# The triangular inverses' substitution on GpSimd instead of VectorE, in an encoder trunk with three mixers

## The chip, the cores and the metric

One core of one Trainium2 chip runs the whole kernel. The metric is the device time of one execution in microseconds, as the median of several runs. The engines are TensorE (PE, with its weight loads PEld), VectorE (DVE), ScalarE (ACT), GpSimd (POOL) and the DMA queues (SP issues them).

## The reference

One layer of a trunk on 1024 tokens of width 1024. A normalised and modulated input is projected by one wide matrix (82 tiles of 128 columns). Three branches read the projection: an mLSTM matrix memory, a Hyena long convolution, and RWKV-7 time mixing. Each has a gate; the three are projected, merged and projected again. What matters here is the third:

```
def step(state, inp):                       # per head, 64 x 64 state, 16 heads, both directions
    r_t, w_t, k_t, v_t, kk_t, a_t = inp
    sa = einsum('bhij,bhj->bhi', state, -kk_t)
    state = (state * w_t[:, :, None, :] + sa[..., None] * (kk_t * a_t)[:, :, None, :]
             + v_t[..., None] * k_t[:, :, None, :])
    return state, einsum('bhij,bhj->bhi', state, r_t)
```

Each token's update reads the state that the one before it left. All is float32.

## The kernel before

The kernel runs in stages: the modulated input is made, then the mLSTM branch, the Hyena branch, the RWKV branch, and the merge with the output projection. The projection is cut into jobs, one for each 128 columns. A job loads its weight tile in four parts (`load_w`): a DMA into `wraw`, a cast to the high half `wh` on ScalarE, and the difference `wl`, the low half, on GpSimd (L334). Its matmuls (`gemm`, L351 to L353) write `pg`, three for each of 8 row blocks and each half of the tokens. There are three `wraw` buffers and four each of `wh` and `wl`, which is one tile's weights. The jobs are handed out piece by piece among the other stages' work.

RWKV does not go token by token. It takes two heads at a time (8 pairs of heads), and of a pair 16 chunks of 64 tokens, forward and backward at once. Within a chunk the dependence of the tokens on each other is a triangular system of 64 by 64. Its inverse is made ahead by `tphase`, for 8 chunks of both directions together (a half, `g`), so there are two calls for each pair and 16 in all. A call works as follows:

- TensorE forms the triangular products `pq`; ScalarE copies the 32 by 32 blocks of the diagonal to `quad` and the block under it to `q21`.
- VectorE transposes `quad` to `Ab` (L1625), so that each of 128 partitions holds one 32 by 32 triangle. A DMA fills `Tb` with identities (L1628).
- The substitution, 31 steps (L1630 to L1636): step `l` makes the outer product `tm` of column `l` of `Ab` with row `l` of `Tb`, and adds it to the rows of `Tb` below. A step has 31 - l rows and l // 2 + 1 columns; the 31 products have 16 to 136 elements each in a partition, 2856 in all. Each product reads what the sum before it wrote, and each sum reads its product.
- VectorE transposes `Tb` back into `t1` and `t2` (L1641, L1644). TensorE then makes the block under the diagonal by two rounds of small products into `pwx`, with a copy `W` between, and ScalarE copies the parts into `tt`.

`scan` (L1740) then goes through the chunks. A step multiplies by the inverse and carries the state on: a group of products into `pch`, a copy `us` on VectorE (L1769), products with `tt`, copies into `SV` on VectorE and ScalarE, products with `B`, two sums `sn` on VectorE, and again copies into `SV`. One `us` thus stands for one step. Half of the chunks' `tt` is used by 8 steps.

Beside the scan, `weave` places the preparation of the next pair (`prep`, which makes `ar` and `bk` from `tmp`, `s`, `a`), the next half's `tphase`, the end of the pair before (`post`) and the projection jobs. Within a `tphase` there is a `yield` after every fifth step of the substitution, and the generators run under a raised priority (`ahead`, 400 places). A scheduler then orders each engine's queue from the dependences, the priorities and its own costs; each queue is worked off strictly in that order.

Of the kernel before, what the change touches and what calls it, by code (L numbers as in the profile page):

```python
# [28 lines left out]
MUL, ADD, SUB, MAX, MIN = ALU.mult, ALU.add, ALU.subtract, ALU.max, ALU.min  # L29
# [256 lines left out]
class Trunk:  # L286
# [1310 lines left out]
    def tphase(self, cx, g):  # L1597

        nc, rp = self.nc, self.rp
        x2 = lambda n: self.ep.tile([128, 16, 32], F32, name=n, tag="x2", bufs=3)
        q, q21 = x2("quad"), self.ep.tile([128, 16, 32], F32, name="q21", tag="q21", bufs=1)
        pq = [x.rearrange("p (c t) -> p c t", t=CL) for x in self.banks("pq")]

        def blocks():

            for d in range(2):
                for c in range(8):
                    bt, al = cx["bk"][g, d, c], cx["ar"][g, d, c]  # L1610
                    for h in range(2):
                        hs = slice(64 * h, 64 * h + 64)
                        yield partial(nc.tensor.matmul, pq[d][64 * h:64 * h + 32, c, :], bt[hs, 0, 0:32], al[hs, 0, :],
                                      start=True, stop=True)
                        yield partial(nc.tensor.matmul, pq[d][64 * h + 32:64 * h + 64, c, 0:32], bt[hs, 0, 32:64],
                                      al[hs, 0, 32:64], start=True, stop=True)
        self.in_turn(blocks())
        for d, ps in enumerate(pq):
            u = slice(d * 8, d * 8 + 8)
            nc.scalar.copy(q[:, u, :], ps[:, :, 0:32])  # L1620
            for h in range(2):
                nc.scalar.copy(q21[64 * h:64 * h + 32, u, :], ps[64 * h:64 * h + 32, :, 32:64])
        yield
        Ab = self.ep.tile([128, 32, 32], F32, name="Ab", tag="Ab", bufs=1)
        nc.vector.transpose(Ab.rearrange("p t (g u) -> p t g u", g=2),  # L1625
                            q.rearrange("p u t -> p t u").unsqueeze(2).broadcast_to([128, 32, 2, 16]))
        Tb = x2("Tb").rearrange("p a b -> p (a b)").rearrange("p (t s) -> p t s", s=16)
        nc.sync.dma_start(Tb, self.A["tinit"])  # L1628
        tm = rp.tile([128, 136], F32, name="tm", tag="tm", bufs=1)
        for l in range(31):  # L1630
            n, m = 31 - l, l // 2 + 1
            x = tm[:, 0:n * m].rearrange("p (a b) -> p a b", b=m)
            self.tt(x, Ab[:, l + 1:32, l].unsqueeze(2).broadcast_to([128, n, m]),
                    Tb[:, l, 0:m].unsqueeze(1).broadcast_to([128, n, m]))
            o = Tb[:, l + 1:32, 0:m]
            self.tt(o, o, x, ADD)  # L1636
            if l % 5 == 4:
                yield
        tt = self.tt_t[g]
        t1 = x2("t1").rearrange("p a b -> p (a b)").rearrange("p (v s) -> p v s", s=16)  # L1640
        nc.vector.transpose(t1.rearrange("p v s -> p s v"), Tb.rearrange("p t s -> p s t"))  # L1641
        t1 = t1.rearrange("p (g u) s -> p u s g", g=2)
        t2 = x2("t2")
        nc.vector.transpose(t2.rearrange("p u (s g) -> p u s g", g=2), t1)  # L1644
        yield

        W = x2("W")
        pw, px = (x.rearrange("p (u t) -> p u t", t=32) for x in self.banks("pwx"))
        r = [slice(64 * h, 64 * h + 32) for h in range(2)]
        self.in_turn(partial(nc.tensor.matmul, pw[64 * h + 32:64 * h + 64, u, :], q21[r[h], u, :], t1[r[h], u, :],  # L1650
                             start=True, stop=True) for u in range(16) for h in range(2))
        for h in range(2):
            r1, r2 = slice(64 * h, 64 * h + 32), slice(64 * h + 32, 64 * h + 64)
            nc.scalar.copy(W[r2], pw[r2])
            nc.scalar.copy(tt[r1, :, 0:32], t2[r1])
            nc.scalar.copy(tt[r2, :, 32:64], t2[r2])
        yield
        r = [slice(64 * h + 32, 64 * h + 64) for h in range(2)]
        self.in_turn(partial(nc.tensor.matmul, px[64 * h:64 * h + 32, u, :], W[r[h], u, :], t2[r[h], u, :],
                             start=True, stop=True) for u in range(16) for h in (1, 0))  # L1660
        for h in range(2):
            r1 = slice(64 * h, 64 * h + 32)
            nc.scalar.copy(tt[r1, :, 32:64], px[r1])
        yield
# [251 lines left out]
```

## Time and profile before

| | |
|---|---|
| median of 3 runs | 2187.35 us (2179.21 to 2191.44) |
| the profiled execution | 2200.05 us; its span 2198.3 us |
| mean granted clock of TensorE | 0.956 |
| busy: PE, DVE, ACT, POOL | 1994.0, 1634.6, 1103.2, 424.3 us |
| products tm, 496 on VectorE | 145.4 us, mean 293 ns |
| sums Tb, 496 on VectorE | 144.2 us, mean 291 ns |
| splits wl, 408 on GpSimd | 371.5 us, mean 915 ns |

The span is from the first to the last instruction of one execution. A group's line gives the source line, the engine, the operation, the tiles written and read, the shape and count; then the busy time and the mean of one, and the idle time of the engine just before its instructions with what ended it. L476 and L473 are helpers for VectorE, so the tiles' names tell what is meant. A row of the timeline starts with the start and the duration in microseconds.

### The profile page before, as it was taken

The numbers are of one execution on the slowest core, as the hardware profiler recorded it, in microseconds if no ns is written. First come the engines' busy times: TensorE is split into PE (matmuls) and PEld (weight loads), VectorE is DVE, ScalarE is ACT, GpSimd is POOL, SyncE is SP. The second block draws the span as 40 slices with busy tenths as digits, with TensorE's granted clock in tenths as the row PEclk, the third lists the DMA queues.
The fourth block names the chain that finished last, engine by engine and source line by source line (L and its number), as shares of the span: only waits on it lengthen the run. The fifth ranks groups of instructions, "written<-read, shape, count | busy, mean of one in ns | idle before, by whom it ended". The sixth has DMA issues, their size and how long they took to land. (4 is left out here: it accounts for less than half of the span.)

```text
span 2198.3 us, 45984 instructions
## 1 busy us (share of the span) xinstructions
PE 1994.0 (91%) x17098; PEld 1509.2 (69%) x17098; DVE 1634.6 (74%) x4754; ACT 1103.2 (50%) x2558; POOL 424.3 (19%) x485
## 2 busy tenths in 40 slices
PE   6999899999989899899989999999898887897998
PEld 4666777787868677666766676666666665675786
DVE  4854999988447947788787888868887888764536
ACT  5557356454242115664665756667466564532221
POOL 2211311122222432311101111111114411010200
PEclk9999999999999999999998999999899998897999
DMA  8211222334465345321322333224143542445623
GB/s 255 70 67 59 78 77 90 112 101 127 143 200 172 119 138 163 124 68 61 130 79 93 117 106 102 92 81 136 52 155 118 187 144 63 159 143 175 196 89 129
DMA packets 169384, 262.19 MB, mean 119 GB/s; under 512 B 17863, under 2 KB 87335, under 8 KB 169160
## 3 DMA queue, kind: packets, MB, share of 16 engines
q1 hardware_dynamic: 169160, 259.25, 36.3%
q8 instruction: 135, 2.21, 0.4%
q14 instruction: 89, 0.73, 0.1%
HBM read 181.06 MB, written 78.12 MB: 118 GB/s over the span
## 5 line engine op out<-in xcount | busy, mean ns | idle before, releaser
L334 POOL TENSOR_TENSOR wl<-wraw,wh 128x256 fp32r<-128x256 f32 x408 | 371.5, 915 | 1488.6 <-ACT wh L333 1464.8
L351 PE MATMUL pg<-hh,wh 128*128 128x512 f32 x1440 | 601.5, 418 | 20.9 <-ACT wh L333 11.8
L352 PE MATMUL pg<-hh,wl 128*128 128x512 f32 x1440 | 594.3, 413 | 16.4 <-POOL wl L334 16.3
L353 PE MATMUL pg<-hl,wh 128*128 128x512 f32 x1440 | 592.4, 412 | 1.9 <-DVE hl L565 1.8
L351 PEld LDWEIGHTS pg<-hh,wh 128*128 128x128 f32 x1440 | 278.7, 194 | 88.9 <-ACT wh L333 15.1
L352 PEld LDWEIGHTS pg<-hh,wl 128*128 128x128 f32 x1440 | 279.3, 194 | 78.0 <-POOL wl L334 22.2
L353 PEld LDWEIGHTS pg<-hl,wh 128*128 128x128 f32 x1440 | 278.1, 193 | 62.0 <-DVE hl L565 2.8
L333 ACT CAST wh<-wraw 128x256 fp32r<-128x256 f32 x408 | 162.7, 404 | 220.6 <-PE pg L353 122.1
L476 DVE TENSOR_TENSOR tm<-Ab,Tb 128x126 f32<-128x126 f32 (+22 forms) x496 | 145.4, 293 | 4.4 <-DMA Tb<-in_tinit 2.7
L476 DVE TENSOR_TENSOR Tb<-Tb,tm 128x126 f32<-128x126 f32 (+22 forms) x496 | 144.2, 291 | 1.9
L473 DVE SCALAR_TENSOR_TENSOR st<-pg,hmu,st 128x511 f32<-128x511 f32 (+1 forms) x130 | 80.9, 636 | 27.9 <-ACT e L424 17.6
L476 DVE TENSOR_TENSOR G<-pgr,gmask 128x512 f32<-128x512 f32 x128 | 85.4, 679 | 17.0 <-PE pgr L398 17.0
L457 ACT ACTIVATE st<-pg 128x512 f32<-128x512 f32 x74 | 44.2, 597 | 99.9 <-PE pg L353 95.0
L1684 ACT COPY G<-ar 64x128 f32<-64x128 f32 x256 | 64.3, 295 | 48.4 <-DVE G L476 46.6
L473 DVE SCALAR_TENSOR_TENSOR st<-st,pg 128x512 f32<-128x512 f32 x80 | 54.3, 679 | 35.7 <-PE pg L353 12.7
L398 PE MATMUL pgr<-ar,bk 64*128 64x128 f32 x896 | 76.9, 287 | 0.0
L141 DVE SCALAR_TENSOR_TENSOR row<-row 64x1 f32<-64x1 f32 x393 | 72.7, 208 | 2.1
L1769 DVE COPY us<-pch 128x128 f32<-128x128 f32 x128 | 36.3, 283 | 45.8 <-PE pch L398 45.5
L395 PEld LDWEIGHTS pch<-SV,G 128*64 128x64 f32 x256 | 25.3, 139 | 65.5 <-ACT SV L1801 52.3
L395 PE MATMUL pch<-SV,G 128*64 128x64 f32 x256 | 43.2, 252 | 27.7 <-ACT SV L1801 26.2
L476 DVE TENSOR_TENSOR dw<-dw,dw 128x512 f32<-128x512 f32 x92 | 67.1, 760 | 0.9
L395 PEld LDWEIGHTS pch<-SV,B 128*64 128x64 f32 x256 | 25.3, 139 | 60.1 <-ACT SV L1776 50.1
(677 smaller groups left out, 4228.4 us busy)
## 6 DMA issues: line engine op xcount, KB each, us to landing
wraw<-in_w_in SPq DMA_DIRECT2D x340, 128.0 KB, 2.3
low<-lora SPq DMA_DIRECT2D x32, 512.0 KB, 4.1
sig<-st SPq DMA_DIRECT2D x48, 256.0 KB, 2.6
st<-sig SPq DMA_DIRECT2D x48, 256.0 KB, 3.5
wraw<-in_w_br SPq DMA_DIRECT2D x68, 128.0 KB, 2.8
adw<-in_ada_w SPq DMA_DIRECT2D x16, 512.0 KB, 7.1
x<-in_x SPq DMA_DIRECT2D x8, 512.0 KB, 6.1
hx<-st SPq DMA_DIRECT2D x16, 256.0 KB, 2.0
```

The source lines that it names most:

```text
L141: self.ops.append(lambda: self.nc.vector.scalar_tensor_tensor(o, a, s, b, op0=op0, op1=op1))
L333: self.nc.scalar.copy(hi, raw)
L334: self.nc.gpsimd.tensor_tensor(lo, raw, hi.bitcast(F32), op=SUB)
L351: nc.tensor.matmul(p, wh, hh, start=(k == 0), stop=False)
L352: nc.tensor.matmul(p, wl, hh, start=False, stop=False)
L353: nc.tensor.matmul(p, wh, hl, start=False, stop=(k == n - 1))
L395: ins = f()
L398: ins = f()
L457: self.nc.scalar.activation(o, p, AF.Tanh, scale=0.5)
L473: return self.nc.vector.scalar_tensor_tensor(out, in0, s, in1, op0=op0, op1=op1)
L476: return self.nc.vector.tensor_tensor(out, a, b, op=op)
L1684: nc.scalar.copy(G[0:64, :, d, h, 0:64], cx["al"][g, d, b % 4][hsl[h]])
```

## The change

The product and the sum of each step are issued on GpSimd and not on VectorE. Nothing else of the source is changed.

```
         for l in range(31):
             n, m = 31 - l, l // 2 + 1
             x = tm[:, 0:n * m].rearrange("p (a b) -> p a b", b=m)
-            self.tt(x, Ab[:, l + 1:32, l].unsqueeze(2).broadcast_to([128, n, m]),
-                    Tb[:, l, 0:m].unsqueeze(1).broadcast_to([128, n, m]))
+            nc.gpsimd.tensor_tensor(x, Ab[:, l + 1:32, l].unsqueeze(2).broadcast_to([128, n, m]),
+                                    Tb[:, l, 0:m].unsqueeze(1).broadcast_to([128, n, m]), op=MUL)
             o = Tb[:, l + 1:32, 0:m]
-            self.tt(o, o, x, ADD)
+            nc.gpsimd.tensor_tensor(o, o, x, op=ADD)
             if l % 5 == 4:
                 yield
```

The scheduler's order of all engines moves with it. On VectorE, the end of the third substitution and the transposes that follow it stood thus before:

```order
L476 TENSOR_TENSOR Tb_10427<-Tb_10427,tm_10429 128x3x15
L476 TENSOR_TENSOR sn_10858<-pch_10774,sn_10722 128x128
L476 TENSOR_TENSOR tm_10429<-Ab_10425,Tb_10427 128x30
L476 TENSOR_TENSOR bk_11068<-a_10997,s_10995 128x4x64
L476 TENSOR_TENSOR Tb_10427<-Tb_10427,tm_10429 128x2x15
L476 TENSOR_TENSOR sn_10858<-sn_10858,pc_9071 128x128
L476 TENSOR_TENSOR tm_10429<-Ab_10425,Tb_10427 128x16
L476 TENSOR_TENSOR hsp_11133<-mm_9628,hsp_11133 128x512
L476 TENSOR_TENSOR Tb_10427<-Tb_10427,tm_10429 128x16
L1800 COPY SV_9264<-sn_10858 64x2x64
L1641 STREAM_TRANSPOSE t1_10702<-Tb_10427 128x16x32
L1769 COPY us_10891<-pch_10882 128x128
```

Here one instruction of other work stood between a product and its sum. The same transpose, with what stands before and behind it in VectorE's queue, now:

```order
L1800 COPY SV_9620<-sn_10444 64x2x64
L476 TENSOR_TENSOR bk_10634<-tmp_10389,s_10386 128x4x64
L476 TENSOR_TENSOR bk_10634<-a_10388,s_10386 128x4x64
L1769 COPY us_10490<-pch_10481 128x128
L476 TENSOR_TENSOR bk_10990<-tmp_10389,s_10386 128x4x64
L476 TENSOR_TENSOR bk_10990<-a_10388,s_10386 128x4x64
L1775 COPY SV_9620<-pch_10481 64x2x64
L1641 STREAM_TRANSPOSE t1_10702<-Tb_10427 128x16x32
L476 TENSOR_TENSOR y_9270<-y_9270,pch_10363 128x64
L1644 STREAM_TRANSPOSE t2_10704<-t1_10702 128x512
L476 TENSOR_TENSOR y_9270<-y_9270,pch_10363 128x64
L476 TENSOR_TENSOR sn_10524<-pch_10481,sn_10444 128x128
```

The transpose into t1 moved to an earlier scan step (sn_10444 is some four steps before sn_10858), and the next step's sum sn_10524 stands behind it. On GpSimd, the splits of two weight tiles and the clearing of `s` stood thus before, near the fifth substitution:

```order
L334 TENSOR_TENSOR wl_12527<-wraw_12524,wh_12526 128x256
L334 TENSOR_TENSOR wl_12533<-wraw_12530,wh_12532 128x256
L334 TENSOR_TENSOR wl_12539<-wraw_12536,wh_12538 128x256
L1555 MEMSET s_11491 128x8
L334 TENSOR_TENSOR wl_12545<-wraw_12542,wh_12544 128x256
L1555 MEMSET s_11959 128x8
L334 TENSOR_TENSOR wl_12877<-wraw_12874,wh_12876 128x256
L334 TENSOR_TENSOR wl_12883<-wraw_12880,wh_12882 128x256
```

and now, with the end of the fifth substitution ahead of them:

```order
L1633 TENSOR_TENSOR tm_12218<-Ab_12214,Tb_12216 128x30
L1636 TENSOR_TENSOR Tb_12216<-Tb_12216,tm_12218 128x2x15
L334 TENSOR_TENSOR wl_12527<-wraw_12524,wh_12526 128x256
L1633 TENSOR_TENSOR tm_12218<-Ab_12214,Tb_12216 128x16
L1636 TENSOR_TENSOR Tb_12216<-Tb_12216,tm_12218 128x16
L334 TENSOR_TENSOR wl_12533<-wraw_12530,wh_12532 128x256
L334 TENSOR_TENSOR wl_12539<-wraw_12536,wh_12538 128x256
L334 TENSOR_TENSOR wl_12545<-wraw_12542,wh_12544 128x256
L334 TENSOR_TENSOR wl_12877<-wraw_12874,wh_12876 128x256
```

The substitution's instructions stand almost without a gap, and most of the splits stand in a row behind its last sum. Over all 16 calls 41 splits stand inside a substitution.

## The prediction

> **What bounds the kernel now.** I read the page's first two parts, then the windows, then the groups, then the substitution on the timeline.
>
> ```profile
> PE 1994.0 (91%) x17098; PEld 1509.2 (69%) x17098; DVE 1634.6 (74%) x4754; ACT 1103.2 (50%) x2558; POOL 424.3 (19%) x485
> ...
> 1000.00:1100.00 100.00, 92.40 (x1055) 68.55 (x1057) 79.59 (x246) 54.32 (x133) 14.33 (x17) 0.93 0.29 94
> 1200.00:1300.00 100.00, 93.15 (x1238) 68.59 (x1234) 87.26 (x264) 66.32 (x164) 13.41 (x19) 1.00 0.32 103
> ```
>
> The two windows lie in the RWKV scan (columns: length, then PE, PEld, DVE, ACT, POOL busy, clock, DMA share, GB/s). TensorE is busy 92 to 93%, but matmul ends are modelled and overlap; its queue still waits for the scan's small steps, which go through VectorE (80 to 87%). GpSimd is idle for 86%. So VectorE's time matters where it delays a scan step, and GpSimd has room on average. Whether it has room where the substitution stands is the question.
>
> ```profile
> L476 DVE TENSOR_TENSOR tm<-Ab,Tb 128x126 f32<-128x126 f32 (+22 forms) x496 | 145.4, 293 | 4.4 <-DMA Tb<-in_tinit 2.7
> L476 DVE TENSOR_TENSOR Tb<-Tb,tm 128x126 f32<-128x126 f32 (+22 forms) x496 | 144.2, 291 | 1.9
> ...
> 946.06 0.20 DVE L476 TENSOR_TENSOR tm<-Ab,Tb 128x31 f32<-128x31 f32 x1
> 976.66 0.70 DVE L476 TENSOR_TENSOR Tb<-Tb,tm 128x16 f32<-128x16 f32 x1
> ...
> 1897.74 0.20 DVE L476 TENSOR_TENSOR tm<-Ab,Tb 128x31 f32<-128x31 f32 x1
> 1937.26 0.17 DVE L476 TENSOR_TENSOR Tb<-Tb,tm 128x16 f32<-128x16 f32 x1
> ```
>
> The 992 instructions that move take 145.4 + 144.2 = 289.6 us, 18.1 us in each of 16 substitutions of 62. Each instruction needs the one before it. The timeline rows are the first and last instruction of the second substitution and of the sixteenth: from 946.06 to 1937.43 stand 15 substitutions and 14 stretches between them. Over all such pairs of rows a substitution lasts 38.0 us on average (it shares VectorE with other work) and a stretch between 30.1 us. A period is 68.1 us; about eight scan steps fall in it.
>
> **The change, part by part.** *Taken off VectorE:* 18.1 us per period. What it is worth depends on the scan step.
>
> ```profile
> 1055.72 0.29 DVE L1769 COPY us<-pch 128x128 f32<-128x128 f32 x1 [2.94 <-PE pch L398]
> 1061.07 0.29 DVE L1769 COPY us<-pch 128x128 f32<-128x128 f32 x1 [0.44 <-PE pch L398]
> ```
>
> A step without a substitution beside it took 5.35 us. With it, 5.3 steps stand in a substitution in the program order before: 38.0 / 5.3 = 7.2 us. So at best 1.8 us a step is to be had, some 9 to 10 us per period.
>
> *Put on GpSimd:* 62 dependent instructions. No small one is in the trace; the nearest are the weight splits of 256 and 512 elements.
>
> ```profile
> L334 POOL TENSOR_TENSOR wl<-wraw,wh x408: 715/742/10347, 34.0 to 2091.0; 128x256 fp32r<-128x256 f32 x136
> L1108 POOL TENSOR_TENSOR hl<-st,hh x16: 1267/1316/2142, 1666.0 to 1729.1; 128x512 fp32r<-128x512 f32 x16
> ```
>
> By the shortest of each (durations are min/median/max in ns), 1267 - 715 = 552 ns for 256 elements: 2.16 ns an element and 163 ns fixed. The 31 products have 2856 elements and the 31 sums as many: 5712 x 2.16 + 62 x 163 = 12.3 + 10.1 = 22.4 us.
>
> *The wait of each on the one before.* GpSimd has one such pair:
>
> ```profile
> 198.87 0.95 POOL L671 MEMSET rm<- 64x1024 f32 x1
> 199.88 0.11 POOL L672 MEMSET rm<- 64x8 f32 x1
> ...
> 1663.57 0.73 POOL L334 TENSOR_TENSOR wl<-wraw,wh 128x256 fp32r<-128x256 f32 x1 [11.27 <-PE ptv L1693]
> 1664.52 1.18 POOL L334 TENSOR_TENSOR wl<-wraw,wh 128x256 fp32r<-128x256 f32 x1 [0.22 <-POOL wl L334]
> ```
>
> The second memset started 0.06 us after the first ended; the split at 1664.52 is put down to the split before it, 0.22 us after its end. Bounds 62 x 0.06 = 3.7 and 62 x 0.22 = 13.6 us. I take 0.10 us, 6.2 us, since the memset pair is the plain case.
>
> *VectorE against GpSimd.* The splits have a maximum of 10.3 us. Where:
>
> ```profile
> 876.89 0.69 DVE L476 TENSOR_TENSOR a<-k,a 128x512 f32<-128x512 f32 x1
> 876.95 5.80 POOL L334 TENSOR_TENSOR wl<-wraw,wh 128x256 fp32r<-128x256 f32 x3 [7.71 <-ACT wh L333]
> 880.33 0.75 DVE L473 SCALAR_TENSOR_TENSOR st<-pg,hmu,st 128x511 f32<-128x511 f32 x1
> 882.18 0.71 DVE L476 TENSOR_TENSOR tm<-Ab,Tb 128x126 f32<-128x126 f32 x1
> ```
>
> Three splits, 2.1 us when alone, took 5.80 us, beside an unbroken run of VectorE instructions with two inputs in SBUF; they got on when VectorE came to one whose input is in PSUM (880.33). And a product on VectorE took 0.71 us beside a split, where the group's mean is 0.29. Each holds the other up. In the changed order the third substitution has beside it, of VectorE work with two SBUF inputs, one scan over s, one tmp, a and mm each, four bk and two sn:
>
> ```profile
> L1564 DVE TENSOR_TENSOR_SCAN s<-smask,s 128x520 f32<-128x520 f32 x32 | 39.7, 1240 | 10.8 <-ACT s L1561 9.8 <-issue 1.0
> L476 DVE TENSOR_TENSOR bk<-a,s 128x256 f32<-128x256 f32 x64 | 29.0, 456 | 0.1
> L476 DVE TENSOR_TENSOR bk<-tmp,s 128x256 f32<-128x256 f32 x64 | 27.2, 430 | 3.9 <-ACT s L1567 3.6
> L473 DVE SCALAR_TENSOR_TENSOR tmp<-a,kk 128x512 f32<-128x512 f32 x32 | 22.6, 707 | 2.8 <-ACT a L1560 2.8
> L476 DVE TENSOR_TENSOR a<-k,a 128x512 f32<-128x512 f32 x32 | 23.3, 727 | 3.7 <-ACT mm L1572 3.6
> 1004.94 0.68 DVE L476 TENSOR_TENSOR mm<-mm,a 128x512 f32<-128x512 f32 x1
> L476 DVE TENSOR_TENSOR sn<-sn,pc 128x128 f32<-128x128 f32 x120 | 37.3, 311 | 0.6
> ```
>
> That is 1.24 + 0.71 + 0.73 + 0.68 + 2 x 0.46 + 2 x 0.43 + 2 x 0.31 = 5.8 us, so GpSimd loses between 0 and 5.8 us; I take 4, since in the rows above it lost the whole run. VectorE's loss falls on work that has slack there.
>
> *What is queued behind.* GpSimd's queue holds 41 splits inside the 16 substitutions, 2.6 each, 1.9 us. The others stand behind the last sum, where before they started between other work. Behind the first product (it waits for the identity's DMA and the transpose to Ab) the same splits stand; the DMA itself stays on SP's queue where it was. Substitution: 22.4 + 6.2 + 4 + 1.9 = 34.5 us, against 38.0 before.
>
> That alone would be a gain of 3.5 us. But the order around it changed too. Between Ab and the transpose to t1, VectorE now has 25 instructions on average instead of 57, and 1.9 scan steps instead of 5.3; the transpose to t1 waits for GpSimd in order, and behind it stand the scan's next steps. TensorE likewise stops at the products into pwx. The other 6.1 steps now stand in the stretch between.
>
> *The stretch between.* TensorE's matmuls from pwx to the next pq, at the spacing of starts in the trace, need 21.3 us in the order before and 28.5 in the new one:
>
> ```profile
> 1003.30 0.39 PE L351 MATMUL pg<-hh,wh 128*128 128x512 f32 x1
> 1003.53 0.39 PE L352 MATMUL pg<-hh,wl 128*128 128x512 f32 x1
> ```
>
> (0.23 us a 512-column matmul; the scan's small ones, timed likewise, make the remainder.) So the stretch grows by at least 7.2 us. At most it grows by 3.3 steps at 5.35 us, 17.7 us. I take 11, nearer the lower end, since a step and the work between pwx and pq overlap in part: 30.1 + 11 = 41.1 us.
>
> *Sum.* 34.5 + 41.1 = 75.6 us against 68.1: 7.5 us more in each of 15 periods, 112 us. The first substitution runs before the scan; I count nothing for it, since the VectorE and TensorE work that stood beside it is there to do either way. The profiled execution took 2200.05 us (span 2198.3 and 1.75 around it), 12.7 over the median of 2187.35; the change's 112 us give 2312 for it and 2300 for the median. From the ends: 22.4 + 3.7 + 0 + 1.9 + 37.3 = 65.3 us a period (42 us faster, 2145) and 22.4 + 13.6 + 5.8 + 1.9 + 47.8 = 91.5 (351 slower, 2538).
>
> **A rule weighed.** For 128x512 with both inputs in SBUF the trace has 1.267 us on GpSimd and 0.69 on VectorE (876.89), 1.84 times. The Trainium skill, GPSIMD Engine Reference, section "Performance versus the Vector engine", gives 1.96 times for such an instruction at 2048 elements; at 512 the trace roughly agrees, and no row here shows it at a hundred. Taken for the small ones too, the page's ratio would make 18.1 x 1.96 = 35.5 us of instructions, an estimate from that page, 13.1 us a period over my 22.4, and 2497 in all. The same page, section "Performance pitfalls for Q7 kernels", has reads with a step over 8 bytes about half dearer per element; the products read Ab by columns, and no run here shows such a read on GpSimd.
>
> **Rivals.**
> - *Faster: the substitution hides.* If wait and blocking cost together little and the scan's steps run at 5.35 us once VectorE is free, a period shrinks by up to 9.5 us: 2187 - 142 = 2045. For it: by the same count of matmuls 25 us of TensorE's work stand beside the substitution in the new order, and 86% of GpSimd is idle. Against it: 62 dependent instructions with a fixed part each. The place is the wait before t1; it decides at a substitution of 27.0 us with my stretch, or at 30.8 with the shortest one.
> - *No change:* the two terms cancel, 2187.
> - *Slower still, the ratio:* GpSimd takes VectorE's time times 1.84 at every size. 18.1 x 1.84 = 33.3, 10.9 us a period more than 22.4: 2300 + 164 = 2464. For it: the ratio is what one size of this trace shows. Against it: two sizes on GpSimd give a fixed part of 163 ns, near the 151 ns of VectorE's shortest product, so small ones should differ less.
> - *Slower still, the splits:* the four or more splits behind the last sum, 4 x 0.74 = 3.0 us, stop the projections' matmuls each time: 45 us more, 2345. For it:
>
> ```profile
> PE pg L352 <- POOL wl L334: 17.3, 15, 6.6
> ```
>
> In this row of the waits TensorE waits 17.3 us for splits in 15 places already. Against it: four wl buffers hold a whole tile.
>
> **How the numbers follow.** Forecast 46% (2215 to 2385), ratio 14%, splits 12%, no change 8%, faster 20%. About 0.5%, 11 us, is what these runs can tell from no change. Faster 0.20, same 0.08, slower 0.72. The range is 2150 to 2465: below it lies half of the faster case, above it half of the ratio's.
>
> **What would show it.** In the changed profile: tm and Tb under POOL with a mean of 0.35 to 0.45 us; POOL busy near 424 + 16 x 26 = 840 us or more; first product to last sum 30 to 40 us; VectorE idle before t1 and released by POOL Tb, 5 us or more each time; TensorE's idle before pwx grown; VectorE's busy time down by up to 290 us. I am wrong if t1 never waits, if the stretch between grows by less than 4 us, or if a small GpSimd instruction takes 0.25 us or 0.6.

## The result, and the profile after

The changed kernel takes 2415.36 us (median; 2410.12 to 2419.59) against 2187.38 us of the kernel before on the same chip: a ratio of 1.1046, 95% interval 1.1007 to 1.1086. It is 228 us slower; the forecast was 112 us slower, so the sign was right and the size less than half of it. The time lies inside the range of 2150 to 2465 us.

The engines' line of the page after:

```profile
PE 1993.9 (83%) x17098; PEld 1503.4 (62%) x17098; DVE 1448.0 (60%) x3762; ACT 1099.5 (46%) x2556; POOL 791.3 (33%) x1477
```

The two windows at the same places as before (length, then PE, PEld, DVE, ACT, POOL busy, clock, DMA share, GB/s):

```profile
1000.00:1100.00 100.00, 72.02 (x852) 52.03 (x851) 51.09 (x118) 44.05 (x108) 45.89 (x99) 0.87 0.19 65
1200.00:1300.00 100.00, 78.67 (x1013) 58.26 (x1011) 54.23 (x120) 51.03 (x122) 33.28 (x74) 0.90 0.29 94
```

And of the groups the two that moved and the transpose behind them (busy time, mean ns, then idle time ahead and what ended it):

```profile
L1633 POOL TENSOR_TENSOR tm<-Ab,Tb 128x126 f32<-128x126 f32 (+22 forms) x496 | 193.0, 389 | 168.1 <-DVE Ab L1625 69.7
L1636 POOL TENSOR_TENSOR Tb<-Tb,tm 128x126 f32<-128x126 f32 (+22 forms) x496 | 202.2, 408 | 36.8
L1641 DVE STREAM_TRANSPOSE t<-Tb 128x512 f32<-128x512 f32 x16 | 16.9, 1059 | 281.6 <-POOL Tb L1636 264.7
```

TensorE is busy 1993.9 us, before 1994.0. The span grew from 2198.3 to 2408.4, so the 210 us are all time in which TensorE stands still. No engine has become the bound; GpSimd is busy a third of the span. The last row tells where to look: VectorE sat idle 264.7 us ahead of the transpose into `t1`, released by the substitution's last sum.

What that does to TensorE is seen on the timeline of after, first VectorE's rows, then TensorE's:

```profile
1089.52 0.74 DVE L473 SCALAR_TENSOR_TENSOR st<-pg,hmu,st 128x511 f32<-128x511 f32 x1
1109.05 1.05 DVE L1641 STREAM_TRANSPOSE t<-Tb 128x512 f32<-128x512 f32 x1 [18.79 <-POOL Tb L1636]
1110.01 0.65 DVE L476 TENSOR_TENSOR hsp<-kk,hsp 128x512 fp32r<-128x512 f32 x1
...
1091.59 0.40 PE L353 MATMUL pg<-hl,wh 128*128 128x512 f32 x1
1110.71 0.80 PE L1433 MATMUL phs<-hsp,ones_r 128*128 128x512 f32 x1 [18.72 <-DVE hsp L476]
```

VectorE comes to the transpose at 1090.3 and stands there for 18.79 us, because `Tb` is not finished on GpSimd. Behind the transpose in its queue is an ordinary difference, `hsp`, which waits for nothing of the substitution. TensorE's next matmul needs that `hsp`, and TensorE's queue is in order too: it stands for 18.72 us, with everything behind `phs`. One instruction queued too early stops two engines. What is late at TensorE is whatever stood behind the transpose that time, as its waits show:

```profile
PE phs L1433 <- DVE hsp L476: 89.1, 7, 18.7
PE pch L395 <- ACT SV L1776: 66.0, 26, 18.4
PE pch L395 <- ACT SV L1801: 61.5, 20, 18.5
PE pch L395 <- DVE us L1769: 40.8, 11, 18.1
PE pch L398 <- DVE SV L1800: 31.6, 3, 16.8
```

Together 289.0 us (columns: total, times, longest). The same rows of before:

```profile
PE phs L1433 <- DVE hsp L476: 4.6, 7, 1.2
PE pch L395 <- ACT SV L1776: 21.3, 30, 1.7
PE pch L395 <- ACT SV L1801: 26.2, 25, 5.4
PE pch L395 <- DVE us L1769: 11.7, 20, 2.6
PE pch L398 <- DVE SV L1800: 1.9, 7, 0.4
```

These are 65.7 us. The difference, 223 us, is about the size of the loss (the two profiled spans differ by 210 us; some other rows became shorter). The stalls themselves say the same: in the 263.4 us for which VectorE stands at `t1` in the second to the sixteenth call, TensorE is busy 38.1 us, so it stands still for 225.3. In the order of VectorE's queue, `t1` of the second to the fifth call stood behind the 8th, 15th, 23rd and 31st `us` before, and behind the 4th, 12th, 19th and 28th now, some four scan steps earlier; its result is needed only at the 9th, 17th, 25th and 33rd.

### The profile page after: what moved, and what is told of

Read it like the earlier page. It is cut to its first block, busy times and chain, and to the rows that moved or that the text cites. A ratio compares the mean times of both kernels' runs of the same rounds, so it can differ in the third digit from the quotient of the medians.

```text
span 2408.4 us, 45997 instructions
## 1 busy us (share of the span) xinstructions
PE 1993.9 (83%) x17098; PEld 1503.4 (62%) x17098; DVE 1448.0 (60%) x3762; ACT 1099.5 (46%) x2556; POOL 791.3 (33%) x1477
## 5 line engine op out<-in xcount | busy, mean ns | idle before, releaser
L334 POOL TENSOR_TENSOR wl<-wraw,wh 128x256 fp32r<-128x256 f32 x408 | 350.1, 862 | 1177.0 <-ACT wh L333 1151.9
L351 PE MATMUL pg<-hh,wh 128*128 128x512 f32 x1440 | 611.9, 425 | 21.4 <-ACT wh L333 14.2
L352 PE MATMUL pg<-hh,wl 128*128 128x512 f32 x1440 | 594.6, 413 | 24.4 <-POOL wl L334 24.4
L351 PEld LDWEIGHTS pg<-hh,wh 128*128 128x128 f32 x1440 | 278.3, 193 | 91.6 <-ACT wh L333 17.7
L1633 POOL TENSOR_TENSOR tm<-Ab,Tb 128x126 f32<-128x126 f32 (+22 forms) x496 | 193.0, 389 | 168.1 <-DVE Ab L1625 69.7
L1636 POOL TENSOR_TENSOR Tb<-Tb,tm 128x126 f32<-128x126 f32 (+22 forms) x496 | 202.2, 408 | 36.8
L1641 DVE STREAM_TRANSPOSE t<-Tb 128x512 f32<-128x512 f32 x16 | 16.9, 1059 | 281.6 <-POOL Tb L1636 264.7
L1655 ACT COPY tt<-t 32x512 f32<-32x512 f32 x32 | 19.7, 616 | 217.6 <-DVE t L1644 217.4
L395 PE MATMUL pch<-SV,B 128*64 128x64 f32 x256 | 43.7, 254 | 66.1 <-ACT SV L1776 66.0
L1433 PE MATMUL phs<-hsp,ones_r 128*128 128x512 f32 x48 | 23.6, 491 | 89.2 <-DVE hsp L476 89.1
```

What stands on the lines that cost most here:

```text
L334: self.nc.gpsimd.tensor_tensor(lo, raw, hi.bitcast(F32), op=SUB)
L351: nc.tensor.matmul(p, wh, hh, start=(k == 0), stop=False)
L352: nc.tensor.matmul(p, wl, hh, start=False, stop=False)
L395: ins = f()
L1633: nc.gpsimd.tensor_tensor(x, Ab[:, l + 1:32, l].unsqueeze(2).broadcast_to([128, n, m]), Tb[:, l, 0:m].unsqueeze(1).broadcast_to([128, n, m ...
L1636: nc.gpsimd.tensor_tensor(o, o, x, op=ADD)
```

## The experiments

All times are medians; each ratio is to runs of the kernel before on the same chip, with its 95% interval. My theory is the one above, called the queue theory: not the substitution's work on GpSimd but the place of what waits for it in the in-order queues makes the loss. The rivals were that GpSimd's work is slow as such, that the two engines disturb each other in SBUF, that the weight splits behind the substitution decide, and that TensorE's granted clock does.

**Holding `t1` back.** The generator of `tphase` goes on to `t1` only once `k + 1` of the 8 `us` copies of the half are issued, and the transpose is issued behind the last of them (`k` stands for the number in each version; for the fifth, `k` is 5 and the transpose is tied to the fifth copy by name):

```
+        if hasattr(self, "us_ins"):
+            while self.us_n % 8 < k:            # k = 6: behind the seventh us
+                yield
...
+        with self.tc.issue_after(self.us_ins.ins) if hasattr(self, "us_ins") else ExitStack():
+            nc.vector.transpose(t1.rearrange("p v s -> p s v"), Tb.rearrange("p t s -> p s t"))
...
-            nc.vector.tensor_copy(us, U)
+            self.us_ins = nc.vector.tensor_copy(us, U)
+            self.us_n = m
```

(The places in `weave` at which `tphase` goes on are made denser at the end of a half, so that it can still finish.) Behind the fifth `us`:

> The substitution stays on GpSimd; the transpose to t1 is held in VectorE's queue behind the scan's fifth copy us of its half, one step later than the scheduler had put it. Queue theory (the loss is VectorE and then TensorE standing still behind a transpose that is queued before GpSimd has finished): VectorE's wait before t1 falls from 18 us to about 11 to 12, 15 times 6 to 7 us, so 2305 to 2325 us. GpSimd theory (the 62 instructions are slow there, and hold VectorE up by the shared access to SBUF, wherever t1 stands): no change within 1%, 2390 to 2440. Splits theory (TensorE lacks wl, which stand behind the substitution): no change either.

Measured: 2386.85 us, 1.0898 (1.0856 to 1.0940). Behind the sixth:

> As before, t1 behind the sixth copy us of its half, two steps later. Queue theory: the wait before t1 about 5 us, 2205 to 2240 us. GpSimd theory and splits theory: 2390 to 2440.

Measured: 2363.36 us, 1.0778 (1.0736 to 1.0819). Behind the seventh:

> As before, t1 behind the seventh copy us of its half, three steps later, where it stood with the substitution on VectorE (there behind the seventh or eighth). Queue theory: the wait before t1 under 2 us on average, and VectorE relieved of 290 us: 2100 to 2200 us, most likely 2150, so below the kernel before. GpSimd theory: above 2350. Splits theory: above 2350, with TensorE's wait for wl grown.

Measured: 2331.59 us, 1.0659 (1.0622 to 1.0697). The same hold in the kernel before, as a control:

> Control: the substitution on VectorE as in the kernel before, with the same hold of t1 behind the seventh copy us. Queue theory: t1 hardly moves (it stood behind the seventh or eighth) and VectorE's chain is in its own queue, so 2165 to 2215 us, as before. If the hold by itself were a gain (a better place for t1 whatever engine works), this one would be faster than before by as much as the GpSimd kernel with the hold.

Measured: 2184.40 us, 0.9991 (0.9967 to 1.0016). The hold itself costs and gives nothing, and with GpSimd's substitution each later place is faster. But the seventh gives 84 us of 228, and I had expected nearly all; none of the three times lies in the range of either theory. One stall takes the place of another: from after over the fifth and the sixth to the seventh, VectorE's idle time ahead of `t1` falls from 264.7 to 135.9, 60.9 and 23.5 us (20.2 of it before the scan), and TensorE's wait for `wl` in the scan grows from 18.2 to 85.6, 109.2 and 130.3 us. TensorE's waits in the scan (856 to 2150 us) of the run with the seventh `us`:

```profile
PE pg L352 <- POOL wl L334: 130.3, 20, 13.1
PE pch L395 <- DVE us L1773: 27.3, 12, 11.9
PE pch L395 <- ACT SV L1781: 14.4, 22, 1.3
PE pch L395 <- ACT SV L1806: 11.8, 16, 7.2
```

The waits behind VectorE are back where they were before (53.5 us in three rows). In their place stands a wait for the low halves `wl` from GpSimd, 130.3 us, of which after had 18.2. (The wait for the DMA of `low` grew too, from 8.3 us before to 27.7. It is back at 4.7 in the run below that moves the splits as well; its cause was not followed up.) One such wait, with the rows of ScalarE, GpSimd and TensorE:

```profile
1081.09 0.42 ACT L333 CAST wh<-wraw 128x256 fp32r<-128x256 f32 x1
...
1097.86 0.40 POOL L1636 TENSOR_TENSOR Tb<-Tb,tm 128x110 f32<-128x110 f32 x1
1098.22 0.73 POOL L334 TENSOR_TENSOR wl<-wraw,wh 128x256 fp32r<-128x256 f32 x1
...
1099.00 0.80 PE L352 MATMUL pg<-hh,wl 128*128 128x512 f32 x1 [9.04 <-POOL wl L334]
```

The split could start at 1081.5, when its cast was done, and starts at 1098.22, behind a run of products and sums in GpSimd's queue. It is the same fault in a second queue. In after it was masked: TensorE stood behind VectorE at that time anyway.

**The splits on VectorE.** The splits made during the scan (164 of 408) go to VectorE:

```
-        self.nc.gpsimd.tensor_tensor(lo, raw, hi.bitcast(F32), op=SUB)
+        (self.nc.vector if getattr(self, "in_scan", False) else self.nc.gpsimd).tensor_tensor(lo, raw, hi.bitcast(F32), op=SUB)
...
+            self.in_scan = True
             run(self.setup(cx[0], 0))
...
+            self.in_scan = False
             run(self.post(cx[n - 1]))
```

Without the hold:

> The kernel after, with the 204 or so low halves wl that are made during the scan put on VectorE instead of GpSimd, so that no wl stands in GpSimd's queue behind a substitution. Two queues can hold TensorE up: VectorE's (t1 queued some 18 us before its inverse is ready, with hsp, us and sn behind it: about 300 us of TensorE's waits in the trace of after) and GpSimd's (wl: 18 us of waits there). Theory 1 (VectorE's queue alone decides in this kernel; wl is masked by it): 2390 to 2425, no change to speak of. Rival (the splits of GpSimd decide, as in the prediction's fourth rival): at least 60 us faster, 2355 or less.

Measured: 2414.35 us, 1.1021 (1.0986 to 1.1057): nothing. With the hold behind the seventh `us`:

> The run that held t1 behind the seventh us (2332) and, with it, wl of the scan on VectorE. In the trace of the former TensorE's waits behind VectorE had almost gone, but its waits for wl of GpSimd had grown from 18 to 130 us. Theory 1 (two queues in a row: the second stall came up when the first was taken away): most of the 130 go, 2195 to 2260, so the two edits give far more together (155 to 220 of the 228 lost) than the sum of each alone (84 and about 0). Rival A (GpSimd and VectorE disturb each other in SBUF, so more work on VectorE does not help): 2320 or more. Rival B (TensorE's granted clock, 0.937 against 0.956, is what is left): 2280 to 2320.

Measured: 2210.96 us, 1.0085 (1.0053 to 1.0116). In the kernel before:

> Control: the kernel before (substitution on VectorE) with the same wl of the scan on VectorE. VectorE is busy 808 of the scan's 991 us and gets about 200 x 0.45 us = 90 us more; TensorE waited only 3 us for wl there. All theories: between no change and somewhat slower, 2180 to 2240. If it is faster by over 1%, the edit has a worth of its own that must be taken off the run with the hold.

Measured: 2189.05 us, 0.9990 (0.9966 to 1.0013). So the splits alone give nothing, the hold alone 84 us, both together 204 of the 228 us, and neither has a worth of its own in the kernel before. That both engines are busy in the faster run speaks against a disturbance in SBUF as the main cost. If the granted clock had been what was left, the time would have been 2280 to 2320; it is not. Moving the splits takes away both their place in GpSimd's queue and their time on GpSimd. No run parts the two; for the place speak the rows at 1081 to 1099 us above, and that GpSimd is busy only 812.5 of 2325.4 us with the hold alone.

**The dose.** Every other substitution, the second half of each pair, on GpSimd and the others on VectorE (`nc.gpsimd if g else nc.vector` at L1633 and L1636), first as scheduled:

> Dose: only the substitution of the second half of each pair of groups (8 of 16 calls) is on GpSimd, the other 8 on VectorE as before. If each call costs its own stall, as theory 1 has it: about half of the 228 us, 2280 to 2320. If the loss comes only when one engine must do every chain in a row (a loop of chain and stretch with no slack): much less than half, 2190 to 2240. If the mere mix of the two engines disturbs both: more than half, over 2330.

Measured: 2264.64 us, 1.0336 (1.0309 to 1.0364), a third of the loss and not the half, between the ranges of two of the explanations. VectorE's idle time ahead of `t1` was half of that in after (135.0 us in 8 places against 264.7 in 15), so the stalls halve but cost less each. A part of that is seen in the trace: TensorE still gets 4.5 us of work done in each of these eight stalls, against 2.5 in those of after, and stands still for 98.8 us in them against 225.3. That is 44%, not a third; the rest was not settled. With the hold, and with hold and splits:

> The same with wl left on GpSimd: VectorE's queue is free, the splits stand behind 8 substitutions and not 16. Theory 1: half of the 2332 - 2211 = 121 us that the splits cost with all 16 calls, 2235 to 2275 (against 2265 for every other call without the hold). If the splits have time to get ahead between two calls on GpSimd, some 65 us apart: 2175 to 2210.

Measured: 2227.01 us, 1.0166 (1.0125 to 1.0208). The splits' part is 47 us against the run below, less than the half of 121 that I had expected; TensorE's wait for `wl` did fall to about half (70.9 us).

> Every other substitution (8 of 16) on GpSimd, t1 held behind the seventh us for all 16, wl of the scan on VectorE: both queues free, and VectorE rid of half of the 290 us (145 less, 75 more for wl). If the two queues are all that the change costs (theory 1): no slower than before, 2165 to 2195, ratio 0.987 to 1.003. If the substitution on GpSimd has a cost of its own per call beside the queues (19 us for 16 calls in the run with both edits): 2195 to 2210. If the relief of VectorE turns into TensorE's time: under 2165.

Measured: 2179.61 us, 0.9948 (0.9927 to 0.9968): no slower than before, as the queue theory has it.

**The last place.** `t1` behind the eighth `us` (`k = 7`), in VectorE's queue behind the 8th, 16th, 24th and 32nd, about where it stood in the kernel before, with the splits on VectorE:

> All 16 substitutions on GpSimd, wl of the scan on VectorE, t1 held one step more, behind the eighth us of its half, the last place ahead of the product that needs tt. Theory 1 (the rest of 19 us is VectorE still standing at t1, 49 us in the trace, of which TensorE feels part): 2185 to 2210. Rival (at the eighth us the inverse is late for TensorE's next half, which then waits for pwx, t2 and tt): 2225 to 2280.

Measured: 2166.63 us, 0.9890 (0.9851 to 0.9929), faster than the kernel before and than both ranges that I had named. Its control, the same two edits with the substitution on VectorE:

> Control for the run that beat the kernel before (2167): the same hold behind the eighth us and the same wl on VectorE, with the substitution back on VectorE. If the 24 us are what GpSimd's substitution gives once neither queue holds TensorE up (VectorE is rid of 290 us): this kernel is no faster than before, 2180 to 2215. If they come from the hold and from wl: 2160 to 2175.

Measured: 2172.79 us, 0.9952 (0.9931 to 0.9973). The control is a little faster than before too. It lies where I had put it if the gain came from the hold and the splits, and the two were on different chips, so this pair does not decide. Both again on one chip:

> All 16 substitutions on GpSimd, t1 behind the eighth us, wl of the scan on VectorE, on one chip with its control. If GpSimd's substitution is worth something once the queues are free: at least 0.4% faster than the control, 2155 to 2175. If nothing: within 0.3% of it.

Measured: 2154.75 us, 0.9854 (0.9817 to 0.9891).

> The control: the same hold and the same wl with the substitution on VectorE. 2165 to 2185 by both; what counts is its distance to the run beside it.

Measured: 2178.61 us, 0.9951 (0.9923 to 0.9979). The intervals are apart: with both queues free, the substitution on GpSimd is 24 us (1.1%) faster than the one on VectorE, and the two edits by themselves give 11 us. Last of all the eighth `us` with the splits left on GpSimd:

> All 16 substitutions on GpSimd, t1 behind the eighth us, wl left on GpSimd. Theory 1 (the splits behind the substitution are the second queue): TensorE waits for wl some 130 us as with the seventh us, and the time is 2285 to 2335, 115 us or more above the same kernel with wl on VectorE. If the place of t1 alone decides: 2165 to 2200.

Measured: 2339.36 us, 1.0692 (1.0653 to 1.0731), just above the range of the first theory, and TensorE waits for the splits (whole span; 141.3 us with the seventh):

```profile
PE pg L352 <- POOL wl L334: 148.0, 35, 13.8
```

The ratios of the kernels with all 16 substitutions on GpSimd:

| `t1` | splits on GpSimd | splits on VectorE |
|---|---|---|
| as scheduled | 1.1046 | 1.1021 |
| behind the seventh `us` | 1.0659 | 1.0085 |
| behind the eighth `us` | 1.0692 | 0.9890, 0.9854 |

The fastest, last row right, is the version to keep. Its engines' line, and the rows with the most of TensorE's waiting over the whole span:

```profile
PE 1977.0 (91%) x17098; PEld 1490.1 (69%) x17098; DVE 1506.6 (70%) x3926; ACT 1100.9 (51%) x2556; POOL 726.3 (34%) x1313
```

```profile
PE pch L395 <- ACT SV L1783: 23.4, 30, 2.0
PE pg L352 <- POOL wl L334: 22.9, 13, 9.1
PE pch L395 <- ACT SV L1808: 21.1, 19, 11.6
```

TensorE is back at 91%. The longest single wait in these rows is 11.6 us, where after had 18.7 and the kernel before 6.6.

## Why the prediction was wrong

**The failed step: the growth of the stretch between, put at 11 us and at 17.7 at most.** The prediction worked it out from TensorE's work. By the order, 28.5 us of it stand from `pwx` to the next `pq`, 7.2 more than before, and the other 25 us beside the substitution, where they were to be done meanwhile. Measured: the stretch lasts 51.6 us on average, 21.5 more than before, above the upper bound too (which by the prediction's own counts of steps, 5.3 less 1.9, would be 3.4 x 5.35 = 18.2). Over 15 substitutions (second to sixteenth), windows from the first product to the last sum; the sum's columns are the windows' length and then each engine's busy time. Before:

```profile
sum 569.95, PE 504.76 PEld 362.47 DVE 519.19 ACT 290.81 POOL 116.67; mean PE 33.65 PEld 24.16 DVE 34.61 ACT 19.39 POOL 7.78
```

After:

```profile
sum 467.60, PE 226.03 PEld 157.50 DVE 154.67 ACT 139.51 POOL 399.67; mean PE 15.07 PEld 10.50 DVE 10.31 ACT 9.30 POOL 26.64
```

The 14 stretches between them, before and then after:

```profile
sum 421.42, PE 391.15 PEld 295.80 DVE 289.15 ACT 302.99 POOL 44.90; mean PE 27.94 PEld 21.13 DVE 20.65 ACT 21.64 POOL 3.21
sum 722.65, PE 655.08 PEld 483.26 DVE 464.87 ACT 455.75 POOL 110.87; mean PE 46.79 PEld 34.52 DVE 33.20 ACT 32.55 POOL 7.92
```

TensorE gets 15.1 us of work done beside a substitution, before 33.7, and not the 25 of the prediction; VectorE 10.3 us. In a period TensorE's work is the same as before (15.1 + 46.8 = 61.9 us against 33.7 + 27.9 = 61.6). So some 19 us of it moved into the stretch, where the prediction had 7.2. The prediction saw that `t1` waits with the scan's next steps behind it, and still counted TensorE's work up to `pwx` as if only `pwx` could stop it. TensorE stops at the first product that needs anything queued behind `t1`. The runs that took the stops away bear this out. With the hold behind the seventh `us` TensorE did 21.8 us beside a substitution:

```profile
sum 488.54, PE 327.08 PEld 229.05 DVE 244.27 ACT 203.80 POOL 420.41; mean PE 21.81 PEld 15.27 DVE 16.28 ACT 13.59 POOL 28.03
```

and with the eighth and the splits on VectorE 30.8:

```profile
sum 499.60, PE 461.73 PEld 330.05 DVE 366.08 ACT 268.41 POOL 428.74; mean PE 30.78 PEld 22.00 DVE 24.41 ACT 17.89 POOL 28.58
```

**The substitution was nearly right.** Forecast 34.5 us, measured 467.60 / 15 = 31.2. The instructions take (193.0 + 202.2) / 16 = 24.7 us a call against 22.4. The wait of each on the one before is about 0.08 us, against 0.10:

```profile
1090.43 0.42 POOL L1633 TENSOR_TENSOR tm<-Ab,Tb 128x120 f32<-128x120 f32 x1
1090.93 0.43 POOL L1636 TENSOR_TENSOR Tb<-Tb,tm 128x120 f32<-128x120 f32 x1
```

The blocking by VectorE, 4 us, did not come about, since VectorE stood still most of the time. It did in part in the fastest version, where VectorE is busy 24.4 us of a substitution and not 10.3: its instructions take 449.5 / 16 = 28.1 us, and the substitution 499.60 / 15 = 33.3 us there. Together, in after: 3.3 us less for the substitution and 10.5 more for the stretch, 7.2 a period, 15 x 7.2 = 108 of the 116 us that were missing.

**What was to be seen.** The means of 389 and 408 ns lie about the forecast of 0.35 to 0.45 us, and VectorE's idle time ahead of `t1` was put at 5 us or more, measured 17.6 (264.7 / 15). GpSimd's busy time is 791 us, not 840. TensorE's idle time ahead of `pwx` did not grow as said: 9.8 us in one place. It stood earlier. None of the three signs of being wrong came: `t1` did wait, the stretch grew by more than 4 us, and the small instructions took about 0.4 us in the mean, neither 0.25 nor 0.6.

**VectorE's relief** was put at 9 to 10 us a period at best. With both queues free it is worth 24 us in all, 1.6 a period.

**The rivals.** The ratio (33.3 us of instructions) falls: 395.2 us on GpSimd against 289.6 on VectorE is 1.36 times, not 1.84. So does the ratio of 1.96 that the Trainium skill's page GPSIMD Engine Reference, section "Performance versus the Vector engine", gives for 2048 elements, for instructions of a hundred. The same page of the Trainium skill, section "Performance pitfalls for Q7 kernels", has reads with an inner step over 8 bytes about half dearer per element. The means (389 ns for the products, 408 for the sums) do not test that: in 29 of the 31 products the column's step of 128 bytes is the outer one, and the inner one repeats an element. Only the first two products, of one column each, have it innermost. In after the second of them (30 elements of one column) takes 0.25 us at least and the thirtieth (also 30 elements, 2 by 15) 0.24, too little to tell. The rival of the splits was wrong in this kernel (2414 with them on VectorE) and right as a mechanism: once `t1` is out of the way they cost 121 us behind the seventh `us` (2331.59 - 2210.96) and 185 behind the eighth (2339.36 - 2154.75). The faster rival named the wait before `t1` as the place where it is decided. That was the place; but its condition, a substitution of 27.0 or 30.8 us at most, was not what decided, for the fastest version has a longer one (33.3 us) than after (31.2).

What stays open: why half of the calls cost a third of the loss, and the 11 us that the hold behind the eighth `us` and the splits give with the substitution on VectorE.

## What to carry to other kernels

When work moves to another engine, look where its consumer now stands in its own queue: an instruction that waits there holds up everything behind it, and every engine that needs any of that. A stall can mask a second one of the same kind, so one edit alone may show nothing; test the suspects together as well as one by one, with the same edits in the kernel before as a control. Here one edit of the order, and moving the splits out of the way, turned a loss of 10% into a gain of 1 to 1.5%, of which the two edits alone, with the substitution on VectorE, give 0.5%.

## What the runs showed of the hardware

After such a stall TensorE's clock is low. Three windows of after, around the one at 1091.6 (the last three numbers are granted clock, DMA share, GB/s):

```profile
1091.50:1110.00 18.50, 0.48 (x3) 0.05 (x1) 0.95 (x1) 0.00 (x0) 14.70 (x39) 0.57 0.03 7
1110.00:1114.50 4.50, 3.79 (x34) 3.02 (x34) 2.59 (x7) 3.12 (x5) 0.00 (x0) 0.50 0.36 89
1114.50:1128.00 13.50, 12.95 (x96) 9.58 (x95) 9.91 (x18) 10.43 (x25) 3.07 (x3) 0.99 0.49 166
```

For 4.5 us behind the stall the granted clock is 0.50, then 0.99. It is 0.50 in the 4.5 us behind each of the 15 stalls, and the mean of the kernel falls from 0.956 to 0.923. TensorE is busy 3.79 us of the 4.5 here, so by an estimate half of that, 1.9 us, is what the clock adds to the stall. The 15 periods do not show it: TensorE's busy time in a period is 61.9 us against 61.6 before. The clock rose again with the stalls gone (0.954 with the seventh `us` and the splits moved, 0.969 with the eighth), so the clock went with the stalls; a cause apart from them was not seen. The Trainium skill, TensorE: Matmul & The Clock Gate, section "Part 1: The HAM clock gate (the "warmup" mystery)", has it that an idle TensorE falls to half of its clock and gets the whole back after some 3.4 us of work; the 0.50 and the 4.5 us agree with that, roughly.

GpSimd's small instructions became slower as VectorE became busier beside them: 193.0 + 202.2 = 395.2 us in after, and in the fastest version

```profile
L1638 POOL TENSOR_TENSOR Tb<-Tb,tm 128x126 f32<-128x126 f32 (+22 forms) x496 | 227.0, 458 | 38.2
L1635 POOL TENSOR_TENSOR tm<-Ab,Tb 128x126 f32<-128x126 f32 (+22 forms) x496 | 222.5, 449 | 276.5 <-DVE Ab L1627 124.9 <-DMA Tb<-in_tinit 31.1 <-DVE sn L476 29.8
```

449.5 us, 14% more for the same instructions.
